# Gate and up projections of two feed-forward layers as seven block products in place of eight

## The chip, the cores and the metric

One core of a Trainium2 chip runs the whole program in one launch. The metric is the device time of an execution in microseconds (us), the median of three runs. Matrix products run on TensorE (PE); elementwise work on VectorE (DVE), ScalarE (ACT) and GpSimd (POOL); loads are issued by SyncE (SP). Each engine takes its instructions in a fixed order and waits at the head of its queue.

## The reference

Two decoder layers on 512 tokens of width 1024, in float32. Each layer is a mixing sub-layer (attention heads) and a feed-forward sub-layer, each with a norm before and after. The change is in the feed-forward:

```python
def swiglu(h, w_gate, w_up, w_down):
    return (jax.nn.silu(h @ w_gate) * (h @ w_up)) @ w_down
```

with `h` 512 x 1024 (normed), `w_gate` and `w_up` 1024 x 2816, `w_down` 2816 x 1024.

## The kernel before

**Matrix products.** Every float32 operand is split into a high part (a cast to fp32r on ACT) and a low part (the rest, a subtraction on DVE; `split`, L107). A product is then three matmuls (`mm3`, L190): high by high, high by low, low by high. The stationary operand is 128 x 128; the moving one has up to 512 columns.

**Gate and up.** The 2816 columns are 22 blocks `f` of 128. For each block the gate weights (128 x 1024 elements, one 512 KB load) and the up weights come in turn; `proj` (L202) makes 8 x 3 matmuls of 512 token columns into one PSUM bank `pg`. `tail` (L339) takes silu on ACT, multiplies with the up result on DVE and splits the product into `gh`/`gl` (or `gph`/`gpl`), what the down projection needs. The first four weight blocks are done by `split_start` (L321) in two halves of 256 token columns (`pf`), and between them stand the last two blocks of transposes `tp` of the normed input (`prenorm`, L259), because token blocks 2 and 3 come out of the mixing sub-layer last.

**Down.** `out_rows` (L297) multiplies the 22 blocks by the rows of `w_down` into eight banks `y`; the last six rows are done token block by token block, so that `postnorm` and `prenorm` of the next sub-layer can start early.

**Order.** Weights come through one list `items`; `weights()` (L183) prepares `AHEAD` = 2 items before the one in use: a load on SP into `raw` (4 buffers), the cast `whi` on ACT, the subtraction `wlo` on DVE (8 buffers `wt`, four pairs). The order of each engine's queue is set by a scheduler from the order of the code and priorities (`tc.high_priority`).

Of the kernel before, what the change touches and what calls it, by code (L numbers as in the profile page):

```python
# [41 lines left out]
def tile_trunk(ctx: ExitStack, tc: tile.TileContext, d: dict, out: bass.AP):  # L42
# [290 lines left out]

    def ffn(hT, later, gpost, then):
        NC_ = 14
        gT = [None] * NFF
        pages = {}

        def tail(f, pg, pu):  # L339
            t = temp("sg", (P, S))  # L340
            nc.scalar.activation(t, pg, AF.Silu)
            nc.vector.tensor_tensor(out=t, in0=t, in1=pu, op=ALU.mult)  # L342
            if f < NC_:
                gT[f] = cell("gh", F32R), cell("gl", F32R)
            else:
                i = (f - NC_) // 4
                if i not in pages:
                    pages[i] = page("gph"), page("gpl")
                gT[f] = part(pages[i], ALL, (f - NC_) % 4, ALL)
            split(*gT[f], t)  # L350

        pss = split_start(4, hT, later)
        tail(0, *pss[0:2])
        tail(1, *pss[2:4])
        for f in range(2, NFF):
            ps2 = [bank("pg", "pa" if f % 2 else "ps") for _ in range(2)]
            for ps in ps2:
                proj(ps, weights(), hT)
            tail(f, *ps2)
# [351 lines left out]

    gfp = load_gain(d["norm_ffn_post"][0])
    g_mix.append(load_gain(d["norm_mix_pre"][1]))
    later = ffn(hf, later, gfp, to_mix)
# [305 lines left out]
```

## Time and profile before

| | |
|---|---|
| median of 3 runs | 1216.38 us (1216.29 to 1217.92) |
| the profiled execution | 1216.32 us, of which the span 1214.7 us |
| PE busy | 1189.9 us (98%), 5824 matmuls |
| PE weight loads busy | 986.9 us (81%) |
| DVE busy | 577.7 us (48%) |
| ACT busy | 494.6 us (41%) |
| POOL busy | 95.2 us (8%) |
| DMA | 112.76 MB, 28% of the queues' time |

A matmul's duration runs from its start to the end of its last result, and neighbours overlap; what a matmul costs in a row of them is read from start to start. The same holds for DVE: an instruction starts a little before the one ahead of it has ended.

### The profile page before, as it was taken

The page shows a single profiled execution, that of the slowest core. Times are in us where ns is not written, and L with a number is a line of the kernel's source. Part 1 is how long each engine was busy: PE and PEld are TensorE (multiplying, and loading weights), DVE is VectorE, ACT ScalarE, POOL GpSimd, SP SyncE. Part 2 cuts the span into 40 slices and gives each one's busy share as a digit, 9 for nine tenths or more (in the row PEclk, how much of TensorE's full clock was granted, in tenths as well). Part 3 has the DMA queues.
Part 4 walks back from the last instruction along what each step waited for, and adds up shares of the span by engine and source line. Part 5 has one row for each costly group of instructions (what it writes and reads, how often), then busy time and mean ns, then how long its engine had stood idle before and what let it go on. Part 6 is the DMA issues. An engine that isn't in the chain of part 4 may idle for free.

```text
span 1214.7 us, 15055 instructions
## 1 busy us (share of the span) xinstructions
PE 1189.9 (98%) x5824; PEld 986.9 (81%) x5824; DVE 577.7 (48%) x1023; ACT 494.6 (41%) x932; POOL 95.2 (8%) x141
## 2 busy tenths in 40 slices
PE   8999999999999999999999988999999999999997
PEld 6787777789888888888889876788988888888886
DVE  5634577764333333323355688876433323332313
ACT  5434477734232322213235676764332322322211
POOL 2000024110000000000010212421000000000000
PEclk9999999999999999999999999999999999999999
DMA  6322121413323232334403213131233232332301
GB/s 238 128 89 84 35 71 53 148 62 104 98 94 104 88 104 92 100 103 136 144 1 122 70 54 105 36 106 66 78 99 104 88 104 89 102 98 93 125 31 70
DMA packets 32761, 112.76 MB, mean 93 GB/s; under 512 B 4753, under 2 KB 4913, under 8 KB 32690
## 3 DMA queue, kind: packets, MB, share of 16 engines
q1 hardware_dynamic: 32690, 111.80, 28.2%
q8 instruction: 46, 0.75, 0.3%
q14 instruction: 25, 0.20, 0.1%
HBM read 109.69 MB, written 2.10 MB: 92 GB/s over the span
## 4 chain that ended last, share of the span: by engine, by line
PE 88%; DVE 6%; ACT 4%; issue 1%; POOL 0%; DMA 0%; DVEq 0%; POOLq 0%; SPq 0%; ACTq 0%
PE pg L194 12%; PE pg L193 12%; PE pg L192 12%; PE y L193 9%; PE y L194 9%; PE y L192 9%; PE pf L193 2%; PE pf L194 2%; PE pf L192 2%; PE sc L392 1%; ACT p L397 1%; PE avt L404 1%; PE tp L271 1%; PE pq L192 1%; DVE p L395 1%
## 5 line engine op out<-in xcount | busy, mean ns | idle before, releaser
L108 ACT CAST whi<-raw 128x1024 fp32r<-128x1024 f32 (+2 forms) x211 | 198.3, 954 | 491.5 <-PE pg L193 300.1
L109 DVE TENSOR_TENSOR wlo<-raw,whi 128x1024 fp32r<-128x1024 f32 (+2 forms) x210 | 230.1, 1110 | 321.3 <-ACT whi L108 314.4
L192 PE MATMUL pg<-hf1h,whi 128*128 128x512 f32 x320 | 124.6, 389 | 0.0
L193 PE MATMUL pg<-hf1l,whi 128*128 128x512 f32 x320 | 124.6, 389 | 0.0
L193 PE MATMUL pg<-hf0l,whi 128*128 128x512 f32 x320 | 124.6, 389 | 0.0
L192 PE MATMUL pg<-hf0h,whi 128*128 128x512 f32 x320 | 124.6, 389 | 0.0
L194 PE MATMUL pg<-hf1h,wlo 128*128 128x512 f32 x320 | 124.6, 389 | 0.0
L194 PE MATMUL pg<-hf0h,wlo 128*128 128x512 f32 x320 | 124.6, 389 | 0.0
L342 DVE TENSOR_TENSOR sg<-sg,pg 128x512 f32<-128x512 f32 x40 | 27.5, 688 | 135.8 <-PE pg L194 135.8
L193 PE MATMUL y<-wlo,gh 128*128 128x512 f32 x224 | 87.2, 389 | 0.0
L192 PE MATMUL y<-whi,gh 128*128 128x512 f32 x224 | 87.2, 389 | 0.0
L194 PE MATMUL y<-whi,gl 128*128 128x512 f32 x224 | 87.2, 389 | 0.0
L244 POOL TENSOR_TENSOR rs<-ms,mhalf 128x1 f32<-128x1 f32 x32 | 17.7, 554 | 816.0 <-DVE ms L242 816.0
L193 PEld LDWEIGHTS pg<-hf1l,whi 128*128 128x128 f32 x320 | 60.1, 188 | 12.5
L193 PEld LDWEIGHTS pg<-hf0l,whi 128*128 128x128 f32 x320 | 60.1, 188 | 12.5
L192 PEld LDWEIGHTS pg<-hf0h,whi 128*128 128x128 f32 x320 | 60.1, 188 | 12.5
L192 PEld LDWEIGHTS pg<-hf1h,whi 128*128 128x128 f32 x320 | 60.1, 188 | 12.4
L194 PEld LDWEIGHTS pg<-hf1h,wlo 128*128 128x128 f32 x320 | 60.1, 188 | 12.3
L194 PEld LDWEIGHTS pg<-hf0h,wlo 128*128 128x128 f32 x320 | 60.1, 188 | 12.3
L400 POOL TENSOR_TENSOR p<-p,st 128x128 f32<-128x128 f32 (+1 forms) x64 | 47.3, 747 | 80.0 <-DVE st L414 76.0
L284 ACT ACTIVATE junk<-y 128x512 f32<-128x512 f32 x32 | 19.1, 597 | 80.7 <-PE y L194 79.3
L192 PE MATMUL y<-whi,gph 128*128 128x512 f32 x128 | 50.0, 391 | 0.0
(334 smaller groups left out, 2391.0 us busy)
## 6 DMA issues: line engine op xcount, KB each, us to landing
raw<-in_gu_dram SPq DMA_DIRECT2D x88, 512.0 KB, 3.5
raw<-in_ffn_w_down_dram SPq DMA_DIRECT2D x44, 512.0 KB, 3.5
raw<-in_w0s_dram SPq DMA_DIRECT2D x16, 512.0 KB, 3.5
raw<-in_w1s_dram SPq DMA_DIRECT2D x11, 512.0 KB, 3.5
raw<-in_w0m_dram SPq DMA_DIRECT2D x8, 512.0 KB, 3.6
raw<-in_ab_w_out_dram SPq DMA_DIRECT2D x8, 512.0 KB, 3.5
raw<-in_cd_w_out_dram SPq DMA_DIRECT2D x8, 512.0 KB, 3.5
x<-in_x_dram SPq DMA_DIRECT2D x4, 512.0 KB, 5.7
```

What stands on the lines that cost most here:

```text
L108: nc.scalar.copy(hi, src)
L109: return (eng or nc.vector).tensor_tensor(out=lo, in0=src, in1=hi.bitcast(F32), op=ALU.subtract)
L192: nc.tensor.matmul(ps, wh, xh, start=first, stop=False)
L193: nc.tensor.matmul(ps, wh, xl, start=False, stop=False)
L194: nc.tensor.matmul(ps, wl, xh, start=False, stop=last)
L244: nc.gpsimd.tensor_tensor(out=r, in0=t, in1=mhalf, op=ALU.pow)
L271: nc.tensor.transpose(ps[:, k, :], h[:, tok(4 * i + k)], ident)
L284: nc.scalar.activation(junk, ys[j], AF.Square, scale=1.0 / 32, accum_out=ss[:, i:i + 1])
L342: nc.vector.tensor_tensor(out=t, in0=t, in1=pu, op=ALU.mult)
L392: nc.tensor.matmul(sc, q, k, start=(i == 0), stop=(i == len(ks) - 1))
L395: nc.vector.tensor_tensor_reduce(out=p, in0=sc, in1=tab, scale=1.0, scalar=init, op0=ALU.add, op1=ALU.min, accum_out=neg)
L400: nc.gpsimd.tensor_tensor(out=p, in0=p, in1=r.to_broadcast([P, n]), op=ALU.mult)
```

## The change

The weights of two neighbouring blocks `f` (a pair `p`, 11 pairs per layer) and the input are each cut into 2 x 2: the input by halves of the tokens (256) and of the width (512), the weights by the two blocks and the halves of the width, gate and up together in one 128 x 1024 block. Eight block products become seven, with 15 sums (Strassen's algorithm in Winograd's form). The products of a pair are called by their weights: D1, D2 (weights as loaded), T1, T2 (sums), D3 (as loaded), T3, T4 (sums); their moving operands are A11, A12, S1, R6, S4, R7, A22. Each is 2 x 4 x 3 matmuls of 256 columns into one bank `pp`.

- Input sums (`sums`): out of the transposes, DVE makes S1, R6, S4, R7 and splits seven operands, in place of four; ACT copies A11, A12, A21 first.
- Weight sums (`prep_sum`): T1, T2, T3 on DVE (128 x 1024 each), T4 on GpSimd.
- Result sums (`after`): five on DVE (`comb`, 128 x 512, one input from PSUM), two on GpSimd; then silu and the gate product in halves of 256 tokens.
- The split for the down projection (`ready`) is made in the down stage.
- The first two D1, two D2 and the third D1 run first; the token blocks' late transposes stand in the first D1 and behind the second D1. From product 16 of a layer on, the queues of DVE, ACT, GpSimd and SP are in the order of the code (`tc.manual_schedule`). Weights are prepared three products ahead; the subtraction for the low part is put one product later (`due`, `settle`).

```diff
+AHEAD_SUM = 3
+FETCH_SUM = 5
...
+    OPS = ("D1", "D2", "T1", "T2", "D3", "T3", "T4")
+    order = [(p, o) for p in range(2) for o in OPS[:2]] + [(2, "D1")] + [(p, o) for p in range(2) for o in OPS[2:]]
+    order += [(p, o) for p in range(2, NFF // 2) for o in OPS if (p, o) != (2, "D1")]
...
+        if op == "D1":
+            st["D1"] = block(0, "gain" if p == 2 else "raw")
+        elif op == "D2":
+            st["D2"] = block(1, "gain" if p >= 2 else "raw")
+        elif op == "T1":
+            if p == 0:
+                blocks[l] = page("sum", F32)
+            t = [blocks[l][:, 2 * i:2 * i + 2, :].rearrange("p a b -> p (a b)") for i in range(2)]
+            st["T"], st["X"] = t[p % 2], temp("x") if p else t[1]
+            nc.sync.dma_start(st["X"], d["gu"][l, p, 2])
+        elif op == "T2":
+            st["D3"] = block(3, "raw")
+        return st
+
+    def prep_sum(st, op):
+        def add(o, a, b, eng=nc.vector):
+            eng.tensor_tensor(out=o, in0=a, in1=b, op=ALU.add)
+
+        if op == "T1":
+            add(st["T"], st["D1"], st["X"])
+        elif op == "T2":
+            add(st["T"], st["T"], st["D3"])
+        elif op == "D3":
+            add(st["D2"], st["T"], st["D2"], nc.gpsimd)
+        elif op == "T3":
+            add(st["X"], st["X"], st["D3"])
+        hi, lo = (sb.tile([P, DM], F32R, name=nm, tag="wt", bufs=WT) for nm in ("whi", "wlo"))
+        src = st[{"T1": "T", "T2": "T", "T3": "X", "T4": "D2"}.get(op, op)]
+        nc.scalar.copy(hi, src)
+        due.append(lambda: nc.vector.tensor_tensor(out=lo, in0=src, in1=hi.bitcast(F32), op=ALU.subtract))
...
+    def ahead(i):
+
+        return i + AHEAD_SUM < len(items) and all(isinstance(x[0], int) and x[1] > 1 for x in items[i:i + AHEAD_SUM + 1])
...
     def weights():
...
+        if isinstance(items[i][0], int):
+            settle()
+            fetch(i + 1 + FETCH_SUM)
+            fill(i + 1 + AHEAD_SUM)
+            if not ahead(i):
+                settle()
...
+    def sums(tb, ps, hS):
...
+        if tb < 2:
+            for i, nm in enumerate(("A11", "A12")):
+                put(nm, ps[i])
+                hS[nm, tb] = copy("a1", ps[i])
+            return
+        a11, a12 = (hS.pop((nm, tb - 2)) for nm in ("A11", "A12"))
+        a21 = copy("a2", ps[0])
+        s1, r6 = cell("s1", shape=(P, 4, P)), cell("r6", shape=(P, 4, P))
+        sub(s1, a21, ps[1])
+        sub(r6, s1, a11)
+        put("S1", s1)
+        put("R6", r6)
+        put("A22", ps[1])
+        sub(a12, a12, r6, ALU.add)
+        put("S4", a12)
+        sub(a11, a11, a21)
+        put("R7", a11)
...
+        def product(p, op):
+            w = weights()
+            x = hS[{"D1": "A11", "D2": "A12", "T1": "S1", "T2": "R6", "D3": "S4", "T3": "R7", "T4": "A22"}[op]]
+            ps = bank("pp", "ps" if op in ("T1", "D3") else "pa", (P, 2, 2 * P))
+            for i in range(2):
+                for k in range(4):
+                    mm3(ps[:, i, :], part(w, ALL, i, k, ALL), (x[:, 0, k, :], x[:, 1, k, :]), k == 0, k == 3)
+                if op == "D1" and p < 2 and i == p:
+                    later.pop(0)()
+            return ps
...
+        def gate(out, c):
+            turns[1].append(lambda: nc.scalar.activation(c[:, 0, :], c[:, 0, :], AF.Silu))
+            turns[2].append(lambda: nc.vector.tensor_tensor(out=out, in0=c[:, 0, :], in1=c[:, 1, :], op=ALU.mult))
...
+            elif op == "D3":
+                c12 = half("c12")
+                comb(c12, c[5], q, ALU.add)
+                nc.gpsimd.tensor_tensor(out=c12, in0=c12, in1=c[1], op=ALU.subtract)
+                g[2 * p + 1] = cell("g")
+                gate(g[2 * p + 1][:, T0], c12)
+            elif op == "T3":
+                comb(c[1], c[1], q, ALU.add)
+                nc.gpsimd.tensor_tensor(out=c[5], in0=c[5], in1=c[1], op=ALU.subtract)
+                gate(g[2 * p + 1][:, T1], c[5])
...
+        def run(some):
+            for p, op in some:
+                q = product(p, op)
+                after(p, op, q)
+                turn()
+
+        n = 2 * len(OPS) + 1
+        run(order[:n])
+        with tc.manual_schedule(engines={nc.vector.engine, nc.scalar.engine, nc.gpsimd.engine, nc.sync.engine}):
+            run(order[n:])
+        for _ in range(2):
+            turn()
+
+        def ready(b):
+
+            pages = {}
+            while len(gT) < min(NFF, b + 1 + AHEAD):
+                f = len(gT)
+                if f % 4 == 0:
+                    pages[0] = ready.pages = page("gph"), page("gpl")
+                gT.append(part(ready.pages, ALL, f % 4, ALL))
+                split(*gT[f], g[f])
```

**DVE in the middle of gate/up.** Before, in layer 0 (`wlo`: low part of a weight block; `sg`: silu times up; `gl`: low part for the down projection):

```order
L109 TENSOR_TENSOR wlo_2837<-raw_2834,whi_2836 128x1024
L342 TENSOR_TENSOR sg_2825<-sg_2825,pg_2764 128x512
L109 TENSOR_TENSOR wlo_2867<-raw_2864,whi_2866 128x1024
L109 TENSOR_TENSOR gl_2829<-sg_2825,gh_2828 128x512
L109 TENSOR_TENSOR wlo_2906<-raw_2903,whi_2905 128x1024
```

After, one pair there, from the sum behind T4 of pair 2 on (`q1`, `q5`, `c11`, `c12`: results; `g`: gate product; `sum`, `x`: weight sums, then their low parts):

```order
L464 TENSOR_TENSOR q1_2738<-q1_2738,pp_3257 128x512
L473 TENSOR_TENSOR g_3217<-c12_3214 128x256
L223 TENSOR_TENSOR wlo_3255<-sum_2509,whi_3254 128x1024
L210 TENSOR_TENSOR sum_2509<-sum_2509,raw_3219 128x1024
L473 TENSOR_TENSOR g_3217<-q5_3146 128x256
L223 TENSOR_TENSOR wlo_3288<-sum_2509,whi_3287 128x1024
L464 TENSOR_TENSOR c11_3349<-q1_3315,pp_3324 128x512
L473 TENSOR_TENSOR g_3111<-q1_2738 128x256
L223 TENSOR_TENSOR wlo_3322<-raw_3219,whi_3321 128x1024
L210 TENSOR_TENSOR x_3184<-x_3184,raw_3219 128x1024
L223 TENSOR_TENSOR wlo_3358<-x_3184,whi_3357 128x1024
L464 TENSOR_TENSOR q1_3315<-q1_3315,pp_3394 128x512
```

and its rest, with the low parts of the next pair's D1 and D2 and its first weight sum:

```order
L473 TENSOR_TENSOR g_3351<-c11_3349 128x256
L223 TENSOR_TENSOR wlo_3392<-raw_3151,whi_3391 128x1024
L464 TENSOR_TENSOR c12_3452<-q5_3385,pp_3427 128x512
L223 TENSOR_TENSOR wlo_3425<-raw_3354,whi_3424 128x1024
L464 TENSOR_TENSOR q1_3315<-q1_3315,pp_3462 128x512
L223 TENSOR_TENSOR wlo_3460<-raw_3389,whi_3459 128x1024
L210 TENSOR_TENSOR sum_2509<-raw_3354,x_3422 128x1024
```

Where two weight blocks took four rows, seven products take 19.

**GpSimd at the same place**, which had nothing there before; `raw_3151` is the weight sum of pair 3, `c12` and `q5` are result sums of pairs 2 and 3:

```order
L501 TENSOR_TENSOR c12_3214<-c12_3214,q1_2738 128x512
L506 TENSOR_TENSOR q5_3146<-q5_3146,q1_2738 128x512
L210 TENSOR_TENSOR raw_3151<-sum_2509,raw_3151 128x1024
L501 TENSOR_TENSOR c12_3452<-c12_3452,q1_3315 128x512
L506 TENSOR_TENSOR q5_3385<-q5_3385,q1_3315 128x512
```

Three sums a pair are now on this engine, one of 128 x 1024 and two of 128 x 512.

**DVE where token block 3 arrives.** Before, from its residual sum `x3` over its norm (`t`) to the splits `hf0l` and the first `wlo`:

```order
L292 SCALAR_TENSOR_TENSOR x3_64<-t_2478,rs_2485,x3_64 128x512 x2
L242 TENSOR_SCALAR ms_2492<-ss_2490 128x1
L265 SCALAR_TENSOR_TENSOR t_2478<-x3_64,rs_2494,gain_2122 128x1024
L109 TENSOR_TENSOR hf0l0_2126<-tp_2589,hf0h0_2124 128x4x128
L109 TENSOR_TENSOR hf0l1_2127<-tp_2596,hf0h1_2125 128x4x128
L109 TENSOR_TENSOR hf0l0_2126<-tp_2627,hf0h0_2124 128x4x128
L109 TENSOR_TENSOR hf0l1_2127<-tp_2634,hf0h1_2125 128x4x128
L109 TENSOR_TENSOR wlo_2516<-raw_2513,whi_2515 128x1024
```

After, from the first result sum on (`t` is the same norm):

```order
L464 TENSOR_TENSOR c11_2610<-q1_2577,pp_2585 128x512
L342 TENSOR_TENSOR a1_2397<-a1_2397,a2_2542 128x512
L368 SCALAR_TENSOR_TENSOR t_2482<-x3_64,rs_2498,gain_2122 128x1024
L223 TENSOR_TENSOR wlo_2582<-raw_2507,whi_2581 128x1024
L111 TENSOR_TENSOR sR7_2562<-a1_2397,sR7_2562 128x4x128
L223 TENSOR_TENSOR wlo_2615<-sum_2509,whi_2614 128x1024
L342 TENSOR_TENSOR s1_2655<-a2_2653,tp_2648 128x512
L210 TENSOR_TENSOR sum_2509<-sum_2509,raw_2579 128x1024
L342 TENSOR_TENSOR r6_2656<-s1_2655,a1_2455 128x512
L464 TENSOR_TENSOR c11_2704<-q1_2671,pp_2679 128x512
L111 TENSOR_TENSOR sS1_2548<-s1_2655,sS1_2548 128x4x128
```

Sums, splits and low parts now stand ahead of the norm and behind it, up to S1, without which T1 can't start.

**DVE a little later**, in pairs 0 and 1: gate products of pair 0 (`g_2841`) ahead of low parts of pair 1 (`wlo_2810` for T1, `wlo_2844` for T2), and a weight sum of pair 2:

```order
L464 TENSOR_TENSOR c12_2838<-q5_2773,pp_2813 128x512
L210 TENSOR_TENSOR sum_2509<-raw_2503,x_2741 128x1024
L473 TENSOR_TENSOR g_2841<-c12_2838 128x256
L210 TENSOR_TENSOR x_2741<-x_2741,raw_2776 128x1024
L464 TENSOR_TENSOR q1_2577<-q1_2577,pp_2847 128x512
L223 TENSOR_TENSOR wlo_2810<-sum_2509,whi_2809 128x1024
L473 TENSOR_TENSOR g_2841<-q5_2773 128x256
L210 TENSOR_TENSOR sum_2509<-sum_2509,raw_2776 128x1024
L464 TENSOR_TENSOR q1_2577<-q1_2577,pp_2880 128x512
L210 TENSOR_TENSOR sum_2509<-raw_2507,x_2944 128x1024
L223 TENSOR_TENSOR wlo_2844<-sum_2509,whi_2843 128x1024
```

A gate product here stands ahead of work for the next products, though it is itself the last link behind a GpSimd sum and a silu.

## Rows read from the trace of the kernel before

**Rows 1.** The page, the chain that ended last: its shares by engine
```profile
PE 88%; DVE 6%; ACT 4%; issue 1%; POOL 0%; DMA 0%; DVEq 0%; POOLq 0%; SPq 0%; ACTq 0%
```

**Rows 2.** Stretches gate/up of layer 0, layer 1: from:to length, busy us (instructions), clock, DMA
```profile
266.47:508.85 242.38, 242.38 (x1169) 205.01 (x1168) 86.52 (x96) 73.58 (x96) 1.09 (x2) 1.00 0.30 98
846.07:1088.45 242.38, 242.38 (x1169) 205.05 (x1169) 86.58 (x96) 73.61 (x95) 1.09 (x2) 1.00 0.30 96
```

**Rows 3.** PE in order of time: start us, us, what; 24 matmuls apart
```profile
379.65 0.39 PE L192 MATMUL pg<-hf0h,whi 128*128 128x512 f32 x1
385.09 0.39 PE L192 MATMUL pg<-hf0h,whi 128*128 128x512 f32 x1
```

**Rows 4.** PE in order of time, first four blocks of layer 0
```profile
266.47 0.28 PE L192 MATMUL pf<-hf0h,whi 128*128 128x256 f32 x1
273.67 1.03 PE L271 MATMUL tp<-ident,t 128*128 128x128 f32 x8
274.46 0.36 PE L192 MATMUL pf<-hf0h,whi 128*128 128x256 f32 x1
```

**Rows 5.** DVE in order of time: three pairs of neighbours
```profile
379.35 1.23 DVE L109 TENSOR_TENSOR wlo<-raw,whi 128x1024 fp32r<-128x1024 f32 x1
380.49 0.68 DVE L109 TENSOR_TENSOR gl<-sg,gh 128x512 fp32r<-128x512 f32 x1
...
695.63 0.69 DVE L109 TENSOR_TENSOR ptl<-pt,pth 128x512 fp32r<-128x512 f32 x1 [0.92 <-ACT pth L108]
696.24 0.47 DVE L395 CUSTOM_DVE_ANT_0 p<-sc,tabc,negsink 128x256 f32<-128x256 f32 x1
...
787.67 0.42 DVE L109 TENSOR_TENSOR ptl<-pt,pth 128x256 fp32r<-128x256 f32 x1
788.01 0.28 DVE L395 CUSTOM_DVE_ANT_0 p<-sc,tabD 128x128 f32<-128x128 f32 x1
```

**Rows 6.** ACT groups by shape: count, busy us, mean ns
```profile
L108 ACT CAST whi<-raw 128x1024 fp32r<-128x1024 f32 x163 | 170.8, 1048 | 482.6 <-PE pg L193 300.1 <-PE y L193 109.0 <-PE pf L193 18.5
...
L341 ACT ACT_TABLE_LOAD x2 | 2.6, 1283 | 0.0
```

**Rows 7.** POOL: one group by shape, and one instruction in order of time
```profile
L109 POOL TENSOR_TENSOR wlo<-raw,whi 128x1024 fp32r<-128x1024 f32 x1 | 2.4, 2380 | 0.1
...
699.51 1.04 POOL L798 TENSOR_TENSOR p<-p,rden 128x512 f32<-128x512 f32 x1 [8.52 <-ACT z L732]
```

**Rows 8.** DVE and POOL in order of time, where both work on SBUF
```profile
689.26 0.83 DVE L741 SCALAR_TENSOR_TENSOR z<-z,gl,rl 128x512 f32<-128x512 f32 x1 [0.62 <-ACT rl L739]
...
689.50 1.49 POOL L798 TENSOR_TENSOR p<-p,rden 128x512 f32<-128x512 f32 x1
...
690.01 1.52 DVE L741 SCALAR_TENSOR_TENSOR z<-z,gl,rl 128x512 f32<-128x512 f32 x1
...
785.57 0.83 POOL L400 TENSOR_TENSOR p<-p,st 128x384 f32<-128x384 f32 x1 [1.40 <-DVE st L414]
...
785.65 1.29 DVE L109 TENSOR_TENSOR mixdl<-u,mixdh 128x512 fp32r<-128x512 f32 x1 [0.16 <-ACT mixdh L108]
```

**Rows 9.** Handing on from DVE to ACT, and from ACT to DVE
```profile
253.70 1.28 DVE L292 SCALAR_TENSOR_TENSOR x<-t,rs,x 128x1024 f32<-128x1024 f32 x1 [0.66 <-POOL rs L244]
...
255.02 1.06 ACT L262 ACTIVATE t<-x 128x1024 f32<-128x1024 f32 x1 [2.23 <-DVE x L292]
...
285.55 1.05 ACT L108 CAST whi<-raw 128x1024 fp32r<-128x1024 f32 x1
...
286.62 1.23 DVE L109 TENSOR_TENSOR wlo<-raw,whi 128x1024 fp32r<-128x1024 f32 x1 [0.20 <-ACT whi L108]
```

**Rows 10.** DVE in order of time: pre-norm of token blocks 2 and 3
```profile
265.10 1.29 DVE L265 SCALAR_TENSOR_TENSOR t<-x,rs,gain 128x1024 f32<-128x1024 f32 x1 [0.66 <-POOL rs L244]
...
268.33 1.42 DVE L292 SCALAR_TENSOR_TENSOR x<-t,rs,x 128x512 f32<-128x512 f32 x2
...
271.77 1.29 DVE L265 SCALAR_TENSOR_TENSOR t<-x,rs,gain 128x1024 f32<-128x1024 f32 x1 [0.66 <-POOL rs L244]
```

More of the change, by code (lines that the diff above doesn't have):

```diff
@@ L170, in tile_trunk, with settle, load_sum, block @@
     used = [0]
+    blocks = {}
+    due = []
+    def settle():
+        while due:
+            due.pop(0)()
+    def load_sum(l, p, op):
+        st = blocks.setdefault((l, p), {})
+        def block(i, tag):
+            t = sb.tile([P, DM], F32, name="raw", tag=tag, bufs={"raw": RAW, "gain": 2}[tag])
+            nc.sync.dma_start(t, d["gu"][l, p, i])
+            return t
+        if op == "D1":
[26 more added lines that the diff above has]
+        due.append(lambda: nc.vector.tensor_tensor(out=lo, in0=src, in1=hi.bitcast(F32), op=ALU.subtract))
+        return tuple(t.rearrange("p (a k m) -> p a k m", a=2, m=P) for t in (hi, lo))
     def fetch(n):
         while len(raws) < min(n, len(items)):
-            raws.append(load(*items[len(raws)]))
+            it = items[len(raws)]
+            raws.append(load_sum(*it) if isinstance(it[0], int) else load(*it))
     def fill(n):
@@ L295, in postnorm, with out_rows @@
         return t
-    def out_rows(nblk, lhs, finish):
+    def out_rows(nblk, lhs, finish, ready=lambda b: None):
         RES = res(nblk)
@@ L302, in out_rows @@
             w = weights()
+            ready(b)
             for tb in range(NT):
@@ L307, in out_rows @@
         ws = [weights() for _ in range(RES)]
+        ready(nblk - 1)
         later = []
@@ L331, in store, with ffn, comb, half @@
         return lambda: None
[L334 to L344, printed above, removed]
-            else:
[L346 to L359, printed above, removed]
+    def ffn(hS, later, gains, then):
+        g = [None] * NFF
+        gT = []
+        st = {}
+        def product(p, op):
[8 more added lines that the diff above has]
+            return ps
+        def comb(out, a, b, op):
+            with tc.high_priority():
+                nc.vector.tensor_tensor(out=out, in0=a, in1=b, op=op)
+        def half(name):
+            return cell(name, shape=(P, 2, 2 * P))
+        turns = [[], [], []]
+        def gate(out, c):
+            turns[1].append(lambda: nc.scalar.activation(c[:, 0, :], c[:, 0, :], AF.Silu))
+            turns[2].append(lambda: nc.vector.tensor_tensor(out=out, in0=c[:, 0, :], in1=c[:, 1, :], op=ALU.mult))
+        def turn():
+            turns.append([])
+            for fn in turns.pop(0):
+                fn()
+        T0, T1 = slice(0, 2 * P), slice(2 * P, S)
+        def after(p, op, q):
+            c = st.setdefault(p, {})
+            if op == "D1":
+                c[1] = half("q1")
+                nc.scalar.copy(c[1], q)
+            elif op == "D2":
+                c11 = half("c11")
+                comb(c11, c[1], q, ALU.add)
+                g[2 * p] = cell("g")
+                gate(g[2 * p][:, T0], c11)
+            elif op == "T1":
+                c[5] = half("q5")
+                nc.scalar.copy(c[5], q)
+            elif op == "T2":
+                comb(c[1], c[1], q, ALU.add)
[6 more added lines that the diff above has]
+            elif op == "T3":
+                comb(c[1], c[1], q, ALU.add)
+                nc.gpsimd.tensor_tensor(out=c[5], in0=c[5], in1=c[1], op=ALU.subtract)
+                gate(g[2 * p + 1][:, T1], c[5])
+            else:
+                comb(c[1], c[1], q, ALU.add)
+                gate(g[2 * p][:, T1], c[1])
+        def run(some):
[17 more added lines that the diff above has]
+                split(*gT[f], g[f])
+        gs = gains()
@@ L361, in finish @@
         def finish(tb, ys):
-            return then(tb, postnorm(tb, ys, gpost, then is store))
-        return out_rows(NFF, lambda b, tb: part(gT[b], ALL, tok(tb)), finish)
+            return then(tb, postnorm(tb, ys, gs, then is store))
+        return out_rows(NFF, lambda b, tb: part(gT[b], ALL, tok(tb)), finish, ready)
     def halves(a):
@@ L710, in to_mix, with gains0 @@
         return prenorm(tb, [(g_mix[0], ALL)], hTs[0], "ps", t)
[L712 to L714 removed]
+    def gains0():
+        g = load_gain(d["norm_ffn_post"][0])
+        g_mix.append(load_gain(d["norm_mix_pre"][1]))
+        return g
+    later = ffn(hf, later, gains0, to_mix)
     hT = hTs[0]
```

38 lines of the change are left out of this document (28 added, 10 removed).

## The prediction

> **What bounds the kernel now.** I read the chain of waits first: PE holds 88% of it [rows 1], and POOL and DMA are put at 0%. Then the two stretches of gate/up by engine: PE is busy for all of their 242.38 us, DVE for 86.5, ACT for 73.6, POOL for 1.1, at a granted clock of 1.00, the upper level of 2.4 GHz [rows 2]. So this stage is a row of matmuls, and its price is their number times their spacing. The reader is to see the spacing in PE's order of time: 24 matmuls of 512 columns take from 379.65 to 385.09 us, 5.44 us, 0.2267 each [rows 3]. Matmuls of 256 columns already stand in the first four blocks: 60 from 266.47 to 273.67 us, 0.120 us each [rows 4]. Half the columns cost 53% of the time, so cutting the tokens in two gives back a part of what the missing product saves.
>
> **The floor that PE sets.** After, a layer has 11 x 7 x 24 = 1848 matmuls of 256 columns, 1848 x 0.120 = 221.8 us, and two groups of transposes that take 0.79 us each from PE (273.67 to 274.46, [rows 4]): 223.3 us for 242.38, or 19.0 us less a layer and 38.1 for both. The Trainium skill, "TensorE: Matmul & The Clock Gate", section "Back-to-back issue gap", gives 262 cycles for 256 columns, 109 ns; by an estimate from that the products would take 201.7 us. The row shows 120 ns in the same form of work, so the row is used.
>
> The trace of before tells nothing of seven products with sums behind them, since no such sum runs there. What can eat the 19.0 us is DVE, in whose queue one pair now has 19 instructions for 7 x 24 x 0.120 = 20.16 us of PE.
>
> **DVE's own work in a pair.** From start to start a 128 x 1024 subtraction takes 1.14 us, 512 elements take 0.61, 256 take 0.34 [rows 5]. A pair has ten of the first (seven low parts, three weight sums), five result sums and four gate products: 11.4 + 3.05 + 1.36 = 15.8 us, under 20.16.
>
> **Waits for ACT inside DVE's queue.** T3's low part stands right behind T3's sum but needs ACT's cast between them. The sum lasts 1.23 us; handing over costs about 0.04 each way (253.70 + 1.28 to 255.02, and 285.55 + 1.05 to 286.62, [rows 9]); the cast takes 1.05 [rows 6]. From the sum's start that makes 2.36 us in place of 1.14: 1.22 us of wait. T1's low part has 0.95 us of other work in between, and waits 0.27. Together 1.5 us. ACT itself has seven such casts a pair, 7.4 us, and smaller copies, and is no bound.
>
> **GpSimd's sums.** DVE and GpSimd work in turns where DVE reads two SBUF operands: the first `z` ends at 690.09, the second at 691.53 instead of 0.61 later, since a GpSimd instruction ran between them; `mixdl` takes 1.29 us in place of 0.68 behind one that had started 0.08 us ahead [rows 8]. From `z` to `z` 1.44 us pass, so a GpSimd instruction that lasts 1.04 alone [rows 7] costs DVE 0.83. In the new queue all but the five result sums read two SBUF operands. The 1024 sum on GpSimd was measured once, 2.38 us [rows 7], so it costs DVE 2.18, and it comes right when T2's low part is due. For its 512 sums the ends are 0.83 held (the row with one operand spread out, 1.04 us) and 1.08 (half of 2.38, with its start, 1.28 us). The one behind T3 costs all of it; the one behind D3 runs beside a result sum of 0.61, and 0.22 to 0.47 remain.
>
> The Trainium skill, "SBUF — State Buffer", section "Who interferes with whom", says that such an instruction and a GpSimd one that reads SBUF exclude each other for the whole instruction, and that whoever issues first decides. The trace agrees on the exclusion, with 0.2 us less than the whole instruction; held for all of it the three would cost 0.6 us more a pair.
>
> **Sum for a pair.** 15.8 + 1.5 + 2.18 + (0.83 to 1.08) + (0.22 to 0.47) = 20.5 to 21.0 us, against 20.16 of PE. From below, all of GpSimd's time could fall into times when DVE waits for PE, and the pair would stay at 20.16; from above, with whole GpSimd instructions and 0.1 us for each of six hand-overs, 22.2. I take 20.8: DVE sets the pace, PE waits 0.6 us a pair, and it waits at T2, whose low part is the one behind GpSimd. Before, a pair's four blocks took 4 x 5.44 = 21.76.
>
> **The start of a layer.** Here I follow DVE's queue with the same prices, on the clock of before.
> - The transposes of token block 2 are wanted 1.44 us into the stage (half a product), at 267.9. Their norm ended at 266.4 before [rows 10]; two weight sums that now stand ahead put it near 267.2. No wait.
> - Those of block 3 are wanted behind 3 products, the first transposes and 4 matmuls: 266.47 + 8.64 + 0.79 + 0.48 = 276.4. Their norm ended at 273.06 before, the residual sum ahead of it at 269.75 [rows 10], near 270.0 now. Between the two stand nine more instructions of 512 elements, 5.5 us, and with the norm's 1.29 that makes 277.0. PE waits 0.7.
> - T1 of pair 0 is wanted at 266.47 + 14.4 + 1.58 + 0.7 = 283.1. S1 of token block 3 comes, from 277.0 on, behind three instructions of 1024, with itself five of 512, and what a result sum doesn't cover of the first GpSimd sum: 277.0 + 3.4 + 3.05 + 1.57 = 285.0. Wait 1.9. ACT's table load (1.28 us, [rows 6]) falls into this stretch and is covered.
> - T2 of pair 0 waits 0.6 for its low part, T1 of pair 1 waits 1.3.
> - T2 of pair 1: two gate products stand at the head of DVE's queue and wait for a GpSimd sum and then a silu, the second GpSimd sum of 1024 takes its 2.2 us, and a sum for pair 2 stands ahead of the low part. Wait 4.5.
>
> Together 9.0 us; I hold 6 to 11 for possible. Between T2 of pair 1 and T2 of pair 2 DVE has 10.6 us of work for 17.3 of PE and catches up, so pairs 2 and 3 run without waits, and the pace of 20.8 is paid in pairs 4 to 10: 7 x 0.6 = 4.3 us. At the end three splits for the down projection stand ahead of T3's low part: 0.4. In the down stage these splits (0.61 us each on DVE) lie beside 5.44 us of PE for a block, at no cost; had they no cover, 22 x 0.61 = 13 us a layer. Loads are the same 44 blocks of 512 KB a layer and move as before.
>
> **Sum.** Per layer -19.0 + 9.0 + 4.3 + 0.4 = -5.3 us, for both -10.6. The profiled execution took 1216.32 us, 1.6 of it outside its span; the median is 1216.38, so no correction is due: 1216.3 - 10.6 = 1205.7. I forecast **1206 us**.
>
> **Rivals.**
> - *Covered sums* (17%). GpSimd works while DVE waits for PE anyway, the pair stays at 20.16 and the start costs 3 us: 1216.3 - 38.1 + 6 = 1184. For it: DVE's own work is only 78% of a pair. Against it: the weight sum on GpSimd becomes ready exactly when DVE has work that reads two operands.
> - *DVE and GpSimd as one lane, slower than before* (25%). The pair takes 22.2 us, the start 11.5: 7 x 2.04 + 11.5 + 0.4 = 26.2 us of waits against 19.0, 7.2 a layer more: 1231. It is slower from the point where the waits of a layer pass 19.0 us, for instance a pair of 21.5 us with a start of 9.2. For it: the turns of [rows 8], the long waits that I count at the start already, and many hand-overs between three engines that I price at the least seen. Against it: it needs whole GpSimd instructions and a hand-over price that no row shows.
> - *Waits and gain cancel* (13%): waits of 18 to 20 us a layer, 1214 to 1219.
>
> **How the numbers follow.** The forecast's own case has 45%, with 1196 to 1213 from a start of 6 to 11 us and a pair of 20.5 to 21.1. Within 0.2% (2.4 us) a measurement of this kernel can't tell a change. Faster: 45 + 17 = 62%; the same 13%; slower 25%. The range leaves out half of the first rival below (about 9%) and the end of the second above (about 9%): 1186 to 1228.
>
> **What would show it.** Spacing of the `pp` matmuls: 0.120 us. A pair in the middle of gate/up: 20.5 to 21.0 us, with PE's idle time ahead of T2 (operand R6) and its releaser a DVE low part; if PE has no idle time there, the first rival holds, and with over 21.5 the second. GpSimd's 1024 sum at 2.4 us or, with its own wait, more; DVE low parts behind it lasting 3 us. Idle PE ahead of S1 and R6 of pairs 0 and 1 of some 8 us in sum. No idle PE between the last product and the first `y`. What would make the forecast wrong: a cheaper GpSimd sum, DVE instructions that don't wait for it, or waits for weights that come from loads.

## The result and the profile after

The changed kernel takes 1232.93 us (median of 4 runs, 1232.34 to 1235.5); the kernel before took 1217.15 beside it. The ratio is 1.0134 with a 95% interval of 1.0116 to 1.0151: slower by 1.3%, where 1206 us, 0.9% faster, was forecast, and outside the range of 1186 to 1228. Run once more unchanged it took 1234.58 (ratio 1.0135, 1.0105 to 1.0164).

The page of the changed kernel, against [rows 1], shows that TensorE no longer holds the chain of waits alone.

```profile
PE 1168.7 (95%) x7216; PEld 1032.7 (84%) x7216; DVE 861.5 (70%) x1337; ACT 593.3 (48%) x1110; POOL 244.4 (20%) x207
...
PE 45%; DVE 30%; ACT 9%; issue 9%; POOL 5%; DMA 1%; ACTq 0%; SPq 0%; DVEq 0%; POOLq 0%
DVE wlo L223 9%; PE y L259 8%; PE y L261 8%; PE y L260 8%; DVE sum L210 5%; ACT whi L222 4%; POOL c L501 4%; DVE c L464 2%; DVE x L210 2%; PE sc L568 1%; DVE q L464 1%; ACT p L573 1%; PE avt L580 1%; PE pf L260 1%; PE pq L259 1%
```

PE went from 88% of the chain to 45%, DVE from 6% to 30%, and GpSimd's `c` (the subtraction for c12), which had no counterpart, has 4%.

The windows by stage of the changed kernel, PE alone (length; busy time and matmuls, granted clock, DMA share, GB/s); the second and fourth are gate/up, against [rows 2]:

```profile
0.00:271.36 271.36, 261.56 (x1293) 0.99 0.30 96
271.36:520.18 248.82, 228.81 (x1865) 0.99 0.29 94
520.18:858.11 337.93, 329.21 (x1670) 1.00 0.28 86
858.11:1107.12 249.01, 228.96 (x1866) 0.99 0.28 92
1107.12:1233.80 126.68, 120.20 (x530) 0.99 0.28 91
```

Gate/up takes 248.82 and 249.01 us instead of 242.38 each [rows 2], 13.1 more, where 10.6 less was forecast. Before it the profiled execution lost 4.9 us more (271.36 against 266.47) in code that the change doesn't touch: 1.7 in the first 21 us, where matmuls stand 0.21 us apart for a time instead of 0.12, and 3.1 in two falls of the clock (last section). This execution is also the longest of the four, by 2.6 us; the stages, not the totals, are compared below.

Where PE waits in a steady pair: its rows at T2 (operand `sR`) of the pair that began at 400.84 (start, duration, line, instruction, idle time and its releaser).

```profile
420.17 0.39 PE L261 MATMUL pp<-sR,wlo 128*128 128x256 f32 x1 [1.65 <-DVE wlo L223]
420.39 0.28 PE L259 MATMUL pp<-sR,whi 128*128 128x256 f32 x1
420.51 0.28 PE L260 MATMUL pp<-sR,whi 128*128 128x256 f32 x1
```

The spacing is 0.120 us, as in [rows 4] and as forecast; the one stop costs 1.81 us more than a spacing, and 0.10 more at the next matmul: 1.91. From D3 of one pair to D3 of the next, 22.07 us pass (400.84 to 422.91). That is 20.16 + 1.91, and it is so in pairs 4 to 10 of both layers.

Now DVE's queue over the same pair, the view that explains it:

```profile
400.04 1.21 DVE L210 TENSOR_TENSOR x<-x,raw 128x1024 f32<-128x1024 f32 x1
402.44 1.23 DVE L223 TENSOR_TENSOR wlo<-x,whi 128x1024 fp32r<-128x1024 f32 x1 [1.19 <-ACT whi L222]
403.59 0.68 DVE L464 TENSOR_TENSOR q<-q,pp 128x512 f32<-128x512 f32 x1
404.19 0.42 DVE L473 TENSOR_TENSOR g<-c 128x256 f32<-128x256 f32 x1
404.52 1.22 DVE L223 TENSOR_TENSOR wlo<-raw,whi 128x1024 fp32r<-128x1024 f32 x1
405.66 0.68 DVE L464 TENSOR_TENSOR c<-q,pp 128x512 f32<-128x512 f32 x1
406.25 1.22 DVE L223 TENSOR_TENSOR wlo<-raw,whi 128x1024 fp32r<-128x1024 f32 x1
408.66 0.69 DVE L464 TENSOR_TENSOR q<-q,pp 128x512 f32<-128x512 f32 x1 [1.19 <-POOL c L501]
409.26 1.22 DVE L223 TENSOR_TENSOR wlo<-raw,whi 128x1024 fp32r<-128x1024 f32 x1
410.40 2.32 DVE L210 TENSOR_TENSOR sum<-raw,x 128x1024 f32<-128x1024 f32 x1
412.64 0.68 DVE L464 TENSOR_TENSOR q<-q,pp 128x512 f32<-128x512 f32 x1
413.24 0.41 DVE L473 TENSOR_TENSOR g<-c 128x256 f32<-128x256 f32 x1
413.91 1.23 DVE L223 TENSOR_TENSOR wlo<-sum,whi 128x1024 fp32r<-128x1024 f32 x1 [0.26 <-ACT whi L222]
415.17 1.23 DVE L210 TENSOR_TENSOR sum<-sum,raw 128x1024 f32<-128x1024 f32 x1
416.31 0.42 DVE L473 TENSOR_TENSOR g<-q 128x256 f32<-128x256 f32 x1
417.59 2.52 DVE L223 TENSOR_TENSOR wlo<-sum,whi 128x1024 fp32r<-128x1024 f32 x1 [0.86 <-ACT whi L222]
420.04 0.68 DVE L464 TENSOR_TENSOR c<-q,pp 128x512 f32<-128x512 f32 x1
420.64 0.41 DVE L473 TENSOR_TENSOR g<-q 128x256 f32<-128x256 f32 x1
420.97 1.21 DVE L223 TENSOR_TENSOR wlo<-raw,whi 128x1024 fp32r<-128x1024 f32 x1
422.11 1.21 DVE L210 TENSOR_TENSOR x<-x,raw 128x1024 f32<-128x1024 f32 x1
```

And GpSimd's three instructions in it:

```profile
406.42 2.21 POOL L501 TENSOR_TENSOR c<-c,q 128x512 f32<-128x512 f32 x1 [9.45 <-DVE c L464]
409.49 2.14 POOL L506 TENSOR_TENSOR q<-q,q 128x512 f32<-128x512 f32 x1 [0.86 <-DVE q L464]
416.63 2.41 POOL L210 TENSOR_TENSOR raw<-sum,raw 128x1024 f32<-128x1024 f32 x1 [4.99 <-DVE sum L210]
```

From the first `x` sum at 400.04 to the next at 422.11, 22.07 us pass. The queue stands idle in brackets, and where a duration is twice the usual one the instruction was held by GpSimd. The queue is idle 1.19 and 0.26 for ACT's casts, and 1.19 behind GpSimd's c12 subtraction. `sum<-raw,x` is held for 2.32 - 1.22 = 1.10 by GpSimd's q5 subtraction. At T2's low part DVE is idle 0.86 and then held for 2.52 - 1.22 = 1.30. Together that is 5.9; DVE's own work at the forecast's prices is 15.8, and the 0.4 that is left stands in small gaps. DVE never stands idle for PE: DVE sets the pair, and PE waits for it.

The row to dwell on is 408.66. `q<-q,pp` is the result sum behind T3. It writes in place the cell (`c[1]`) that GpSimd's subtraction at 406.42 reads. That subtraction has itself been held by the low part at 406.25, so it ends only at 408.63, and the sum can't start before. In pair 1, where it started ahead of the low part, the same subtraction took 1.29 us, and it was the low part behind it that was held (2.18 us):

```profile
322.52 1.29 POOL L501 TENSOR_TENSOR c<-c,q 128x512 f32<-128x512 f32 x1 [10.20 <-DVE c L464]
322.72 2.18 DVE L223 TENSOR_TENSOR wlo<-sum,whi 128x1024 fp32r<-128x1024 f32 x1 [0.27 <-ACT whi L222]
```

### The profile page after: what moved, and what is told of

Same layout as the page of the kernel before. It is cut to its first block, busy times and chain, and to the rows that moved or that the text cites. A ratio compares the mean times of both kernels' runs of the same rounds, so it can differ in the third digit from the quotient of the medians.

```text
span 1233.8 us, 18464 instructions
## 1 busy us (share of the span) xinstructions
PE 1168.7 (95%) x7216; PEld 1032.7 (84%) x7216; DVE 861.5 (70%) x1337; ACT 593.3 (48%) x1110; POOL 244.4 (20%) x207
## 4 chain that ended last, share of the span: by engine, by line
PE 45%; DVE 30%; ACT 9%; issue 9%; POOL 5%; DMA 1%; ACTq 0%; SPq 0%; DVEq 0%; POOLq 0%
DVE wlo L223 9%; PE y L259 8%; PE y L261 8%; PE y L260 8%; DVE sum L210 5%; ACT whi L222 4%; POOL c L501 4%; DVE c L464 2%; DVE x L210 2%; PE sc L568 1%; DVE q L464 1%; ACT p L573 1%; PE avt L580 1%; PE pf L260 1%; PE pq L259 1%
## 5 line engine op out<-in xcount | busy, mean ns | idle before, releaser
L111 DVE TENSOR_TENSOR wlo<-raw,whi 128x1024 fp32r<-128x1024 f32 (+2 forms) x122 | 123.9, 1041 | 127.9 <-ACT whi L110 124.7
L260 PE MATMUL pp<-sA,whi 128*128 128x256 f32 x528 | 149.6, 283 | 0.0
L259 PE MATMUL pp<-sA,whi 128*128 128x256 f32 x528 | 149.6, 283 | 0.0
L261 PE MATMUL pp<-sA,wlo 128*128 128x256 f32 x528 | 149.4, 283 | 0.0
L260 PE MATMUL y<-wlo,gph 128*128 128x512 f32 x352 | 137.0, 389 | 0.0
L261 PE MATMUL y<-whi,gpl 128*128 128x512 f32 x352 | 137.0, 389 | 0.0
L261 PE MATMUL pp<-sR,wlo 128*128 128x256 f32 x352 | 103.2, 293 | 30.1 <-DVE wlo L223 29.8
L223 DVE TENSOR_TENSOR wlo<-raw,whi 128x1024 fp32r<-128x1024 f32 x88 | 107.2, 1218 | 6.7 <-ACT whi L222 6.6
L259 PE MATMUL pp<-sR,whi 128*128 128x256 f32 x352 | 101.0, 287 | 2.9 <-ACT whi L222 2.9
L260 PE MATMUL pp<-sS,whi 128*128 128x256 f32 x352 | 99.8, 284 | 2.9 <-DVE sS L111 2.9
L260 PEld LDWEIGHTS pp<-sA,whi 128*128 128x128 f32 x528 | 101.4, 192 | 0.1
L259 PEld LDWEIGHTS pp<-sA,whi 128*128 128x128 f32 x528 | 101.3, 192 | 0.1
L260 PE MATMUL pp<-sR,whi 128*128 128x256 f32 x352 | 100.7, 286 | 0.0
L259 PE MATMUL pp<-sS,whi 128*128 128x256 f32 x352 | 99.8, 284 | 0.3
```

The lines of the kernel that those rows point to most:

```text
L111: return (eng or nc.vector).tensor_tensor(out=lo, in0=src, in1=hi.bitcast(F32), op=ALU.subtract)
L223: due.append(lambda: nc.vector.tensor_tensor(out=lo, in0=src, in1=hi.bitcast(F32), op=ALU.subtract))
L259: nc.tensor.matmul(ps, wh, xh, start=first, stop=False)
L260: nc.tensor.matmul(ps, wh, xl, start=False, stop=False)
L261: nc.tensor.matmul(ps, wl, xh, start=False, stop=last)
```

## Experiments

Theory A says that DVE and GpSimd work in turns, as one lane of 22.07 us a pair. PE waits for as long as this lane exceeds PE's own 20.16, and the lane's terms are those just read, the in-place write among them. There are three rivals. B: GpSimd holds every DVE instruction, whatever it reads, so the shared cell doesn't matter. C: what costs is hand-overs between engines, and GpSimd's time is hidden. D: the pair is held by casts and low parts.

In the table, pair times are from D3 to D3 in pairs 5 to 9 of layer 0. The start loss is the time from the start of the stage to D3 of pair 2, less the 53.4 us that eighteen products and two groups of transposes take. Each ratio is to the kernel before run beside it, which took 1217 to 1218 us every time.

| kernel | median us | ratio to before, 95% | pair us | gate/up, two layers | start loss, layer 0 |
|---|---|---|---|---|---|
| changed kernel | 1232.93 | 1.0134 (1.0116 to 1.0151) | 22.07 | 248.8, 249.0 | 11.2 |
| newcell | 1216.28 | 0.9987 (0.9974 to 0.9999) | 21.30 | 241.2, 242.0 | 9.5 |
| c_dve | 1208.78 | 0.9927 (0.9901 to 0.9953) | 21.16 | 236.6, 236.8 | 6.3 |
| w_dve | 1225.53 | 1.0063 (1.0041 to 1.0085) | 21.89 | 245.1, 245.1 | 9.3 |
| all_dve | 1201.42 | 0.9856 (0.9834 to 0.9878) | 20.97 | 233.2, 232.9 | 4.3 |
| t3_early | 1215.15 | 0.9977 (0.9963 to 0.9990) | 20.80 | 240.4, 240.0 | 12.1 |
| newcell_t3 | 1213.15 | 0.9952 (0.9935 to 0.9969) | 20.54 | 239.0, 239.1 | 12.6 |
| sums_out | 1185.84 | 0.9737 (0.9720 to 0.9753) | 20.16 | 226.3, 226.2 | 2.9 |
| fill | 1190.67 | 0.9775 (0.9755 to 0.9794) | 20.16 | 227.5, 228.9 | 4.2 |
| fill_d2 | 1196.17 | 0.9819 (0.9795 to 0.9843) | 20.16 | 229.9, 231.4 | 6.5 |
| fill_w01 | 1189.48 | 0.9767 (0.9743 to 0.9791) | 20.16 | 227.6, 227.6 | 4.3 |

**newcell: the result sum behind T3 gets a cell of its own.**

```diff
-                comb(c[1], c[1], q, ALU.add)
-                nc.gpsimd.tensor_tensor(out=c[5], in0=c[5], in1=c[1], op=ALU.subtract)
+                c[6] = half("q6")
+                comb(c[6], c[1], q, ALU.add)
+                nc.gpsimd.tensor_tensor(out=c[5], in0=c[5], in1=c[6], op=ALU.subtract)
```

(T4's sum then uses `c[6]` too.)

> The result sum behind T3 writes a cell of its own instead of the one that GpSimd's c12 subtraction still reads. Theory A (DVE and GpSimd are one lane of 22.07 us a pair, and 1.19 us of it is this write waiting for that read): the result sum, which reads one SBUF operand, runs beside the subtraction, and only the low part behind it is held, for about 0.55 us; pair 21.4 us, PE's wait at T2 1.25 instead of 1.91, total 1233 - 2 x 7 x 0.65 - 1 = about 1223 us. Rival B (every DVE instruction is held by a GpSimd one, whatever it reads): the sum waits as long without the shared cell, pair 22.07, total 1233.

The same stretch of this kernel, DVE and then GpSimd:

```profile
419.78 1.22 DVE L223 TENSOR_TENSOR wlo<-raw,whi 128x1024 fp32r<-128x1024 f32 x1
420.91 0.68 DVE L464 TENSOR_TENSOR q<-q,pp 128x512 f32<-128x512 f32 x1
421.51 1.72 DVE L223 TENSOR_TENSOR wlo<-raw,whi 128x1024 fp32r<-128x1024 f32 x1
```

```profile
419.94 2.21 POOL L501 TENSOR_TENSOR c<-c,q 128x512 f32<-128x512 f32 x1 [9.45 <-DVE c L464]
```

The wait of 1.19 is gone. The sum (420.91 to 421.59) runs inside GpSimd's instruction (to 422.15), and only the low part behind it is held, 1.72 - 1.22 = 0.50. The pair is 21.30, as A has it, not B's 22.07. The total fell by more than A's sum, to the time of the kernel before: gate/up is 14.7 us shorter, 14 x 0.77 in the steady pairs, 1.2 at pair 3, and the rest at the starts. The Trainium skill, "SBUF — State Buffer", section "Who interferes with whom", says that a DVE instruction with at most one SBUF input, outside the two-port modes, does not contend with GpSimd. The sum at 420.91 reads one SBUF operand and PSUM, and the trace agrees.

**c_dve, w_dve, all_dve: sums back on VectorE, each in its place.** c_dve moves L501 and L506, w_dve moves only the weight sum, all_dve all three:

```diff
-            add(st["D2"], st["T"], st["D2"], nc.gpsimd)
+            add(st["D2"], st["T"], st["D2"])
...
-                nc.gpsimd.tensor_tensor(out=c12, in0=c12, in1=c[1], op=ALU.subtract)
+                nc.vector.tensor_tensor(out=c12, in0=c12, in1=c[1], op=ALU.subtract)
...
```

> Both result subtractions (c12 and q5, 512 elements) on VectorE instead of GpSimd, the 1024 weight sum stays on GpSimd. Theory A: the lane loses 1.19 + 1.11 and gains 2 x 0.61: pair 20.99 us, total 1233 - 2 x 7 x 1.08 - 1 = about 1217. Rival C (what holds the pair is the hand-over between three engines and the casts in DVE's queue; GpSimd's time is hidden): DVE gets 1.22 us more and nothing back, pair 23.3, total about 1250.

> Only the 1024 weight sum (D2's block plus T) on VectorE, in the place where its instruction stood (behind T2's low part), both result subtractions stay on GpSimd. Theory A: of the 2.16 us that stand at T2's low part, 0.86 is the wait for ACT's cast, which stays, so the lane loses 1.30 and gains 1.14: pair 21.9, total about 1229 to 1231, with less wait at the start. By the price of the prediction (2.18 for the GpSimd sum): pair 22.07 - 2.18 + 1.14 = 21.03, total about 1218. Rival C: pair 23.2, total 1249.

> All three GpSimd sums of a pair on VectorE, each in its place. Theory A: lane 22.07 - 1.19 - 1.11 - 1.30 + 1.14 + 1.22 = 20.83 us a pair, PE still waits 0.67 at T2; with 2 to 3 us less at each layer's start, total 1233 - 17.4 - 5 = about 1211 (1207 to 1215). By the prediction's own prices: 22.07 - 1.19 - 1.11 - 2.18 + 2.36 = 19.95, below PE's 20.16, so PE sets the pair, total about 1202. Rival C: pair 24.4, total 1266.

Pairs of 21.16, 21.89 and 20.97 stand against A's 20.99, 21.9 and 20.83: A holds within 0.17, and rival C, which wanted 23.2 to 24.4, falls. What is missing has a row, in c_dve's queue on DVE:

```profile
414.34 0.68 DVE L464 TENSOR_TENSOR c<-q,pp 128x512 f32<-128x512 f32 x1
415.06 0.69 DVE L501 TENSOR_TENSOR c<-c,q 128x512 f32<-128x512 f32 x1
```

A subtraction right behind the sum whose result it reads starts 0.72 after it instead of 0.60, and a pair has two such places. The totals of c_dve and w_dve lie some 8 and 4 us under A's (1217, 1229 to 1231): their starts lost 6.3 and 9.3 us instead of 11.2, which A's sums for the total hardly counted.

w_dve separates two prices of the weight sum. The prediction took 2.18 us for it on GpSimd. Here it is on DVE and the pair is only 0.18 shorter, where that price gives 1.04. DVE's rows at T2 say why:

```profile
454.06 0.42 DVE L473 TENSOR_TENSOR g<-q 128x256 f32<-128x256 f32 x1
455.34 1.23 DVE L223 TENSOR_TENSOR wlo<-sum,whi 128x1024 fp32r<-128x1024 f32 x1 [0.86 <-ACT whi L222]
456.48 1.22 DVE L210 TENSOR_TENSOR raw<-sum,raw 128x1024 f32<-128x1024 f32 x1
```

With GpSimd quiet (its last sum ended at 449.39), T2's low part still waits 0.86 us, for ACT's cast of the sum just made. Part of GpSimd's time had lain beside this wait, and the prediction's list of casts in DVE's queue lacks it.

In all_dve the total is 1201.42, 1.4% under the kernel before; the expectation by lane (1211) was too high, since the start gained more than I allowed (11.2 to 4.3). That the total meets the 1202 which the prediction's own prices gave is luck: they wanted a pair of 20.16, and it is 20.97.

**t3_early: T3's weight sum one product earlier, nothing else.**

```diff
         elif op == "D3":
             add(st["D2"], st["T"], st["D2"], nc.gpsimd)
-        elif op == "T3":
             add(st["X"], st["X"], st["D3"])
```

> Only T3's weight sum one product earlier in DVE's queue, GpSimd's sums stay as they are. Theory A: of the lane's 22.07 us a pair 1.19 is DVE standing idle until ACT's cast of T3's sum is done, and it goes: pair 20.88, total 1233 - 2 x 7 x 1.19 = about 1216. Rival B (GpSimd's three instructions set the pair and DVE's own idle time lies beside them): pair 22.07, total 1233.

The pair is 20.80, A's 20.88 and not B's 22.07: the 1.19 in front of T3's low part was part of the lane. So D is right about this one term.

**newcell_t3: both edits, all sums still on GpSimd.**

> All three sums stay on GpSimd; the result sum behind T3 has a cell of its own and T3's weight sum stands one product earlier. Theory A (the terms of the lane add): 22.07 - 0.77 - 1.27 = 20.03 us of queue a pair, just under PE's 20.16, so the pair is 20.16 and PE's wait at T2 is gone in the steady pairs; the start keeps about 9.5 us of waits a layer, total about 1202. Rival F (what the one edit frees the other already had): pair 20.8, total about 1212.

This is a miss for A in part: the pair is 20.54, not 20.16, and the total of 1213.15 is near the 1212 of rival F, whose pair was 20.8. The terms don't add to the end. T3's result sum now waits 0.94 us for PE:

```profile
425.06 0.69 DVE L463 TENSOR_TENSOR q<-q,pp 128x512 f32<-128x512 f32 x1 [0.94 <-PE pp L260]
```

while PE stops 0.23 us at D3's operand in each pair, so DVE and PE hold each other by turns. The start lost 12.6 us, and the clock fell there for some 10 us in each layer. newcell alone lost 9.5 there and t3_early 12.1, so the longer start came with the earlier weight sum; by what way, no run isolates.

**sums_out: the three GpSimd sums are left out of the computation.**

> The three sums that stood on GpSimd are left out of the computation, all else in its place. Theory A: lane 22.07 - 1.30 - 1.19 - 1.11 = 18.5 us, PE sets the pair at 20.16, start waits near 4 us a layer: total about 1190 us; that is what the seven products give when no wait is in DVE's queue, and the difference from 1233 is what GpSimd's sums cost. Rival D (the pair is held by casts and low parts, not by GpSimd): pair 21 to 22, total 1215 to 1230.

The total is 1185.84, 4 us under the expectation; half of that is the start, which lost 2.9 a layer and not 4. The pair is 20.16, so D, which wanted 21 to 22, falls as the whole account. Gate/up is 226.25, of which 223.3 is the floor. So the floor of the prediction is real, and what stood on GpSimd, with the waits that it brought, costs 1232.93 - 1185.84 = 47 us.

**fill: all sums on VectorE (the two subtractions as in c_dve), two weight sums moved into the waits for casts.**

```diff
         elif op == "T2":
             add(st["T"], st["T"], st["D3"])
+            add(st["D2"], st["T"], st["D2"])
         elif op == "D3":
-            add(st["D2"], st["T"], st["D2"], nc.gpsimd)
-        elif op == "T3":
             add(st["X"], st["X"], st["D3"])
```

> All sums on VectorE, and two of them moved into the waits for ACT's cast: the weight sum for T4 right behind T2's sum (it fills the 0.86 us before T2's low part), and T3's sum one product earlier (it takes away the 1.19 us before T3's low part). Theory A (only the length of DVE's queue sets the pair): lane 20.97 - 0.86 - 1.19 = 18.9 us, below PE's 20.16, so the pair is 20.16 and PE waits no more at T2: 9.5 us less than all sums on VectorE in place (1201.4), about 1192 us. Rival C (hand-overs between DVE, ACT and PE hold the pair however the queue stands): pair stays near 20.97, total about 1201.

```profile
416.88 1.22 DVE L210 TENSOR_TENSOR sum<-sum,raw 128x1024 f32<-128x1024 f32 x1
418.14 1.22 DVE L210 TENSOR_TENSOR raw<-sum,raw 128x1024 f32<-128x1024 f32 x1
419.29 0.42 DVE L472 TENSOR_TENSOR g<-q 128x256 f32<-128x256 f32 x1
419.62 1.22 DVE L222 TENSOR_TENSOR wlo<-sum,whi 128x1024 fp32r<-128x1024 f32 x1
420.76 1.22 DVE L210 TENSOR_TENSOR x<-x,raw 128x1024 f32<-128x1024 f32 x1
```

These are DVE's rows at T2 of `fill` (its line numbers are one lower from the casts on). The 1024 sum stands where the queue had stood idle, and the low part starts without a bracket. The pair is 20.16 and not C's 20.97, and the total is 1190.67 us where A gave 1192: 2.25% under the kernel before. The three sums on DVE cost 4.8 us in all over leaving them out. DVE is busy 215.6 of 227.5 us and that doesn't matter:

```profile
266.53:494.06 227.53, 224.52 (x1865) 223.70 (x1864) 215.63 (x263) 115.75 (x165) 1.65 (x3) 1.00 0.31 105
```

(length; busy PE, weight loads, DVE, ACT, POOL; clock, DMA share, GB/s.)

**fill_d2 and fill_w01: the start.** The first puts D2 of the third pair ahead of the first T1; the second keeps the T4 weight sum of pairs 0 and 1 where it was.

```diff
-    order = [...] + [(2, "D1")] + [...]
+    order = [...] + [(2, "D1"), (2, "D2")] + [...]
```

> As the kernel with all sums on VectorE and two of them moved (label fill), and D2 of the third pair also ahead of the first T1, so that PE has six products instead of five before it needs the sums of the fourth token block. Theory A (start waits are DVE's queue being late): 2.88 us more cover takes 1.5 to 2.5 us out of each layer's start, total 3 to 5 us below fill, about 1188. Rival E (the block's buffer is still held by a norm's gains, and the load waits): as fill or slower, 1192 to 1200.

> As label fill, but in the first two pairs the weight sum for T4 stands behind T2's low part, where it was, since no wait for a cast is to be filled there. Theory A: T2 of pair 0 gets its low part 1.14 us earlier, 1 to 1.5 us less wait at the start of a layer, total 1188. Rival: the work only moves to the next wait (T1 of pair 1), total as fill, 1190 to 1191.

fill_d2 is 5.5 us slower than fill, in the range that rival E gave. T2's weight sum of pair 0 does wait for its load:

```profile
292.16 2.36 DVE L210 TENSOR_TENSOR sum<-sum,raw 128x1024 f32<-128x1024 f32 x2 [0.75 <-DMA raw<-in_gu_dram]
```

E's reason, a buffer held by a norm's gains, does not hold for this load: SyncE issued it at 288.59, when DVE's weight sum for T1 (287.31) had given its buffer back. And PE stops 1.35 us in a D product at 286.24, for a low part, so the added product brought a late low part of its own. fill_w01 has 1189.48 against 1190.67, inside the spread of either: PE's stop of 1.53 at T2 of pair 0 is gone, 0.72 has come at the low part of D3, and the stop of 0.91 has moved from pair 0 to pair 1. Its rival is right for layer 0 (227.6 against 227.5); what layer 1 gains (227.6 against 228.9) is the fall of the clock that `fill` had there.

**after_again.**

> The changed kernel once more, unchanged: are the places at which TensorE's granted clock fell to its lower level before gate/up (146 to 152 us and 212 to 216 us) its own? If they are chance, this profile has them elsewhere or not at all, and the total stays 1231 to 1236; if they belong to the program, they stand at the same places. The drops behind T2 of pair 1 in both layers (idle 1.6 and 3.2 us ahead of them) are expected again.

It took 1234.58 us. Its clock fell at one of the two places before gate/up and not at the other; the last section has both.

## Why the prediction was wrong

Point by point, its steps against the changed kernel:

- **Floor** (spacing 0.120, 223.3 us a layer): right; sums_out reaches it but for 2.9 us of waits.
- **DVE's own work** (15.8): right, with some 0.4 us of small gaps a pair not counted.
- **Casts in DVE's queue** (1.22 and 0.27): measured 1.19 and 0.26. A third at T2, 0.86, was missing; it lies beside GpSimd's weight sum and adds nothing here, but it stays when that sum goes.
- **The 1024 sum on GpSimd** (2.18): 0.86 + 1.30 = 2.16 at T2, so the size was right, but by luck: only 1.30 of it goes when the sum leaves GpSimd (w_dve), since the rest is also the wait for the cast.
- **q5 behind T3** (0.83 to 1.08): 1.10.
- **c12 behind D3** (0.22 to 0.47): 1.19. **This step failed.** "The one behind D3 runs beside a result sum of 0.61" supposed that the sum may run beside it. It writes the cell that the subtraction reads, so it stands still until the subtraction has ended. With a cell of its own, newcell, the step costs 0.50, nearly what was priced. The code before the run shows both operands (`c[1]` in L501 and in the sum behind T3); I asked which instructions exclude each other by what they read, and not what each one writes.
- **Pair**: 22.07 instead of 20.8; 0.7 to 1.0 of the difference is c12, the rest gaps and q5. Since the queue was priced over PE's 20.16 already, each further 0.1 us is paid 14 times. Pairs 4 to 10 lost 13.4 us a layer, not 4.3, and pair 3 another 0.6.
- **Start** (9.0): 11.2. By place, forecast and measured stop: tb3's transposes 0.7 and 1.07, T1 of pair 0 1.9 and 1.63, T2 of pair 0 0.6 and 0.31 (at D3's first matmul, which stands among T2's), T1 of pair 1 1.3 and 1.12, T2 of pair 1 4.5 and 4.8 (1.61 + 3.19). The walk through the queue was good: these stops make 8.9. Another 1.4 us are matmuls at the clock's lower level behind the last stop, and 0.9 stands at the first transposes and at the matmul behind each stop.
- **End** (0.4): 0.3 to 0.4.
- **Upstream** (nothing changes): the instructions don't, but the profiled execution lost 4.9 us there, 3.1 of them in two falls of the clock.

Sum a layer: -19.0 + 11.2 + 14.0 + 0.4 = +6.6, measured +6.4 and +6.6. The forecast's mechanism was right as far as it went: DVE sets the pair, and PE waits at T2 for a low part. What failed is the size of one of its terms, and the start and the small gaps add to it. With that one write gone (newcell) the kernel takes 1216.28, still 10 us above the forecast: some 7 of them are the pair of 21.30 against 20.8, and 1.7 the starts.

By the prediction's own sign, a pair over 21.5, this is the second rival's case. That rival had the right times (pair 22.2, start 11.5, 1231) for a reason that did not hold: its surplus was to come from longer holds and dearer hand-overs, and most of it (0.7 to 1.0 of 1.3 us a pair) came from one write.

## What to carry to other kernels

When a sum goes to a second engine, list for each instruction behind it on the first engine the cell that it writes: one written in place, and still being read elsewhere, is a wait that a list of which instructions exclude each other does not show, and a fresh cell takes it away (14.7 us of gate/up here). Sums on GpSimd held the VectorE instructions that read two SBUF operands (by 1.10 and 1.30 us), so GpSimd gave no extra lane here; the same sums cost 4.8 us on VectorE once they stood in its waits for casts, and 47 us on GpSimd. Where a queue's length is within a few per cent of the engine that it feeds, price the whole queue with its idle time, since each 0.1 us is paid in every turn of the loop.

## What the runs showed of the hardware

TensorE's granted clock fell in the changed kernel to its lower level (0.50, 1.2 GHz) for some 3 to 4 us at a time. One place is behind the stops of 1.61 and 3.19 us at T2 of pair 1; PE's windows there (busy, matmuls, clock, DMA share, GB/s):

```profile
310.00:312.00 2.00, 0.50 (x2) 1.00 0.00 0
312.00:314.00 2.00, 0.00 (x0) 1.00 0.00 0
314.00:316.00 2.00, 1.40 (x6) 0.57 0.71 205
316.00:318.00 2.00, 2.00 (x13) 0.58 0.17 66
```

The matmuls of 256 columns then stand 0.21 us apart instead of 0.12. all_dve, with no stop longer than 0.91 us there, kept 1.00. `fill` had two stops, 0.91 and 1.53 us, at T2 of pair 0 in both layers, and the clock fell in layer 1 alone. Two more falls stand in code that is the same before and after:

```profile
146.00:148.00 2.00, 2.00 (x9) 0.76 0.75 197
148.00:150.00 2.00, 2.00 (x6) 0.50 0.16 66
...
212.00:214.00 2.00, 2.00 (x7) 0.50 0.00 0
```

The kernel before had 1.00 in both places. The changed kernel run again fell at 146 to 152 once more, not at 212, but at 734, and behind T2 of pair 1 in both layers as before; newcell, fill and fill_w01 fell at neither, all_dve and newcell_t3 at both. Other executions of the kernel before had a mean granted clock down to 0.994, with times up to 1221 us, against 0.999 in the profiled one. So these falls belong neither to the change nor to one program; in the changed kernel they cost 1.6 and 1.5 us, and what decides whether one comes is not settled.
